# A hybrid state space and attention block: the small matmuls of a state space group stand in three portions behind whole weight pieces, and the combination of the dilations takes four steps a head pair

## The chip, the core and the metric

The kernel runs on one NeuronCore of a Trainium2 chip. The time is device microseconds from launch to the last output, the median of repeated runs. The core's engines are TensorE (PE in the profile, PEld for its weight loads), VectorE (DVE), ScalarE (ACT), GpSimd (POOL) and SyncE (SP), which issues most DMAs. Each runs its own list of instructions in order and waits on semaphores for the others.

## The reference

One layer on 512 tokens of width 1024, in fp32. A wide projection feeds a state space branch and an attention branch; both are gated and summed, then come an output projection and a gated feed-forward net. Cut to what the change touches:

```python
xbc = silu(causal_dwconv(xbc, conv_w, conv_b))          # gives xs, B, C
X = (xs * dt).reshape(b, c, Q, G, K, P)                  # 4 chunks of 128 tokens, 8 groups of 4 heads
a_cs = cumsum(dt * A)
CB = einsum('bclgn,bcsgn->bcgls', C, B)
y_diag = einsum('bcgkls,bcsgkp->bclgkp', CB * Ldec, X)   # Ldec: decay between two tokens of a chunk
states = einsum('bclgn,bcgkl,bclgkp->bcgkpn', B, decay_states, X)
prev = scan over chunks of: carry * chunk_decay + states
y_off = einsum('bclgn,bcgkpn,bcgkl->bclgkp', C, prev, exp(a_cs))
y = rms_norm((y_diag + y_off + d_skip * xs) * silu(z))   # per group of 256 channels

# attention: three dilations (1, 4, 16), 8 heads each
wts = softmax(stack(lses), axis=0)
o = einsum('gbsh,gbshd->bshd', wts, stack(outs))         # the combination of the dilations
```

## The kernel before

**Precision by split.** Each fp32 product of a weight and an activation runs as three products of rounded parts: weight high by activation high, high by low, low by high (`mm_chan`, `proj_tok`, `mm_tok`). ScalarE rounds a weight piece to `whi` (line 105), VectorE subtracts for `wlo` (line 106). Weights come in pieces of 512 KB (`raw`, three buffers; `whi` and `wlo` have three each). A piece of the state space stage is 24 matmuls of 128x512, 8 for each of the three products, into a bank `ps_ssd` of the four `mm` banks.

**Large and small work.** The state space stage has 8 groups of 6 pieces: B, C, two of x, two of z. What a group then needs of TensorE beside its pieces, the small work, is in the generator `ssd_side`: `ps_cb` (C by B, 4 matmuls), `ps_bt` (3 transposes of B), `ps_xt` (two banks of 4 transposes of x), `ps_st` (3 matmuls for the states), then for each half j of the group `ps_y` (8 matmuls with 64 columns of weights, the part within a chunk) and `ps_o` (3 matmuls, the part from the state before), and `ps_n` (2 matmuls that sum squares). On the other engines it makes `xdt` and `xdc` (x by time step and by decay, from `ps_xt`), `cbm` (from `ps_cb`, masked), `btok`, `prev` (the running state), the decay matrix in `bc` (a 1 MB load, a subtraction, Relu, Exp, then times `cbm`), y in `ysb`, and `sq`, `sr`, `vv`, `rv` for the norm. After the eighth group come the gates (`ps_gate`, 16 pieces, of which six still carry the last group's small work), the two branch projections (`ps_ap`, `ps_sp`), the output projection and the feed-forward net.

**What sets the order.** TensorE's list is in the order of the code. `tick()` resumes each waiting generator once; there is a tick after the 12th matmul of a piece, inside `mm_chan`, and one at its end. `yield n` in a generator lets n ticks pass. So the numbers in `G0`, `G1`, `GN` (groups 0, 1, and all others), `YL` and `NL` say at which half piece each bit of small work stands. ScalarE's and VectorE's lists are set in this stage by the framework's scheduler from its own estimates. Small work uses the PSUM tags `tr` and `aux`, two banks each; a bank is free again when its reader is done. `bc` and `eb` have two buffers, so `load_decay(g + 2)` (line 777) has to wait until group g's `ps_y` and y are done.

**The combination.** `combine()` weighs the three dilations' outputs for 4 pairs of heads and writes `ah` and `al`, the split input of `ps_ap`. It runs beside the first groups, one tick after the cast to `ah` and one after `al`, so two ticks a pair.

Of the kernel before, what the change touches and what calls it, by code (L numbers as in the profile page):

```python
# [38 lines left out]
def kernel(  # L39
# [6 lines left out]
    nc = tc.nc  # L46
# [556 lines left out]
    def combine():  # L603
# [37 lines left out]
        for j in range(4):  # L641
# [10 lines left out]
            yield 1  # L652
# [43 lines left out]
    def ssd_side(g, bct, xst, zs, at):  # L696
# [12 lines left out]
        yield at["cb"]  # L709
# [7 lines left out]
        btok = T("btok", [P, 3, P])  # L717
        ps = bank("tr", f"ps_bt{g}")
        for c in range(3):
            nc.tensor.transpose(ps[:, c * P:(c + 1) * P], bct[:, 0, c * P:(c + 1) * P], ident)  # L720
        nc.scalar.copy(btok.rearrange("p c n -> p (c n)"), ps[:, :3 * P])
# [3 lines left out]
        xdt = T("xdt", [P, NT, 4, 64])
        xdc = T("xdc", [P, 3, 4, 64])
        for hf in range(2):
            ps = bank("tr", f"ps_xt{g}_{hf}")
            for c in range(2):
                for j in range(2):  # L730
                    o = c * 256 + j * P
                    t0 = (2 * hf + c) * P
                    nc.tensor.transpose(ps[:, o:o + P], xst[:, j, t0:t0 + P], ident)
            p4 = ps.rearrange("p (c h d) -> p c h d", c=2, h=4)
            cc = slice(2 * hf, 2 * hf + 2)
            nc.vector.tensor_mul(xdt[:, cc], p4, dtt[:, cc, hs].unsqueeze(3).broadcast_to((P, 2, 4, 64)))
            n = 2 - hf
            cc = slice(2 * hf, 2 * hf + n)
            nc.vector.tensor_mul(xdc[:, cc], p4[:, :n], dtd[:, cc, hs].unsqueeze(3).broadcast_to((P, n, 4, 64)))
            yield 1  # L740
# [16 lines left out]
        for j in range(2):  # L757
            b = 2 * g + j
            y = ysb[:, b, :]
            psy = bank("aux", f"ps_y{g}_{j}")  # L760
# [5 lines left out]
            pso = bank("aux", f"ps_o{g}_{j}")  # L766
# [9 lines left out]
            yield YL - j  # L776
# [7 lines left out]
        ps = bank("aux", f"ps_n{g}")  # L784
# [17 lines left out]
    normal = dict(zip(("cb", "x", "y"), GN))  # L802
# [6 lines left out]
    for g in range(8):  # L809
        if g > 1:  # L810
            branch_tiles(g)
        if g > 1:
            start(ssd_side(g, *tiles[g], normal), G2W if g == 2 else 0)
        banks = []
        for i in range(6):
# [19 lines left out]
            if (g, i) == (0, 4):  # L835
# [588 lines left out]
```

## Time and profile before

| | |
|---|---|
| median of 3 runs | 1204.27 us (1204.27 to 1204.46) |
| the profiled execution, span within it | 1204.23 us, 1202.3 us |
| busy: TensorE, its weight loads | 1196.1 us (99%), 997.8 us (83%) |
| busy: VectorE, ScalarE, GpSimd | 753.7 us (63%), 575.4 us (48%), 170.5 us (14%) |
| granted clock of TensorE | 0.999 |
| state space pieces, first and last matmul | 263.8 and 595.0 us |
| share of `ps_ssd` in the chain that ended last | 22% |

The busy table gives for each engine the time in which at least one of its instructions runs. The chain that ended last is followed back from the end of the program, at each step to what released it; a row of it has a start, a length and what ran. Rows of the timeline have a start, a length, the engine, the line, output and inputs with their shape, how many instructions were merged, and in brackets how long the engine sat idle before and what ended that. A plain fp32 matmul leaves two records, so `ps_cb L714 x8` is 4 matmuls.

### The profile page before, as it was taken

To read this page: it belongs to the slowest core of one execution; us is meant where nothing else is said; L and a number is where in the kernel's file an instruction comes from. 1 tells how busy PE (TensorE), PEld (TensorE's weight loads), DVE (VectorE), ACT (ScalarE), POOL (GpSimd) and SP (SyncE) were. 2 spreads that over 40 slices of the span, in tenths; PEclk is the share of its full clock that TensorE was granted. 3 is DMA by queue.
4 is the path that set the end of the run, shared out by engine and by line. 5 is a ranking of instruction groups with operands and counts; after the bars stand their busy time and mean duration, and the time that the engine had idled before them with its cause. 6 is when DMAs were issued, how large, how long until landed. Compare 5 with 4: busy or idle time off the path is not lost.

```text
span 1202.3 us, 15963 instructions
## 1 busy us (share of the span) xinstructions
PE 1196.1 (99%) x6316; PEld 997.8 (83%) x6316; DVE 753.7 (63%) x999; ACT 575.4 (48%) x890; POOL 170.5 (14%) x143
## 2 busy tenths in 40 slices
PE   9999999999999999999999999999999999999998
PEld 7877778987888888888888888888888989988887
DVE  6224544467789986877644354654788887885542
ACT  5434565467845657456433324433554445454331
POOL 1034422300000201101011000000223232400000
PEclk9999999999999999999999999999999999999999
DMA  5455544322646444434325332344333332334330
GB/s 187 123 124 128 114 103 107 91 66 74 184 124 200 122 134 124 123 97 115 87 72 144 119 103 90 105 142 157 123 108 103 105 107 85 109 95 168 112 116 35
DMA packets 174955, 138.95 MB, mean 116 GB/s; under 512 B 11552, under 2 KB 149584, under 8 KB 173857
## 3 DMA queue, kind: packets, MB, share of 16 engines
q1 hardware_dynamic: 172001, 131.35, 37.6%
q0 software_dynamic: 2880, 6.59, 2.4%
q8 instruction: 49, 0.80, 0.3%
q14 instruction: 25, 0.20, 0.1%
HBM read 133.22 MB, written 4.70 MB: 115 GB/s over the span
## 4 chain that ended last, share of the span: by engine, by line
PE 99%; ACT 0%; DVE 0%; issue 0%; POOL 0%; DVEq 0%
PE ps_ssd L145 22%; PE ps_qk L145 11%; PE ps_u L1282 10%; PE ps_wd L952 10%; PE ps_gate L145 7%; PE ps_sp L919 7%; PE ps_v L409 6%; PE ps_wo L952 3%; PE ps_ua L1108 2%; PE ps_uc L1108 2%; PE ps_ub L1108 2%; PE ps_u L145 2%; PE ps_ap L145 2%; PE ps_s L537 1%; PE ps_y L764 1%; PE ps_pv L579 1%
## 5 line engine op out<-in xcount | busy, mean ns | idle before, releaser
L106 DVE TENSOR_TENSOR wlo<-raw,whi 128x1024 fp32r<-128x1024 f32 x154 | 194.3, 1263 | 315.2 <-ACT whi L105 217.1
L105 ACT CAST whi<-raw 128x1024 fp32r<-128x1024 f32 x154 | 161.7, 1051 | 308.3 <-PE ps_ssd L145 63.1
L145 PE MATMUL ps_ssd<-hl,whi 128*128 128x512 f32 x384 | 102.9, 397 | 0.0
L145 PE MATMUL ps_ssd<-hh,whi 128*128 128x512 f32 x384 | 98.4, 398 | 0.0
L145 PE MATMUL ps_ssd<-hh,wlo 128*128 128x512 f32 x384 | 95.4, 390 | 0.0
L952 PE MATMUL ps_wd<-whi,asp 128*128 128x512 f32 x336 | 89.8, 389 | 0.0
L145 PEld LDWEIGHTS ps_ssd<-hh,wlo 128*128 128x128 f32 x384 | 72.1, 188 | 15.9
L145 PEld LDWEIGHTS ps_ssd<-hh,whi 128*128 128x128 f32 x384 | 70.6, 188 | 14.0 <-issue 0.2
L145 PEld LDWEIGHTS ps_ssd<-hl,whi 128*128 128x128 f32 x384 | 70.2, 188 | 14.1 <-issue 0.2
L952 PEld LDWEIGHTS ps_wd<-whi,asp 128*128 128x128 f32 x336 | 63.1, 188 | 13.1
L952 PE MATMUL ps_wd<-wlo,asp 128*128 128x512 f32 x168 | 51.7, 389 | 0.0
L556 ACT ACTIVATE s<-s,st 128x128 f32<-128x128 f32 (+1 forms) x96 | 39.8, 417 | 21.6 <-DVE st L550 15.7
L145 PE MATMUL ps_qk<-hh,whi 128*128 128x512 f32 x192 | 49.3, 398 | 0.0
L1156 ACT ACTIVATE facc<-facc 128x512 f32<-128x512 f32 x22 | 13.9, 632 | 71.7 <-DVE facc L52 71.6
L145 PE MATMUL ps_qk<-hl,whi 128*128 128x512 f32 x192 | 47.4, 389 | 0.0
L145 PE MATMUL ps_qk<-hh,wlo 128*128 128x512 f32 x192 | 47.4, 389 | 0.0
L1092 DVE TENSOR_TENSOR ulo<-rawup,uhi 128x1024 fp32r<-128x1024 f32 x31 | 43.5, 1404 | 5.2 <-ACT uhi L1086 5.2
L778 POOL TENSOR_TENSOR sq<-sq 128x512 f32<-128x512 f32 x8 | 12.4, 1550 | 240.5 <-ACT sq L775 240.5
L145 PEld LDWEIGHTS ps_qk<-hh,whi 128*128 128x128 f32 x192 | 35.0, 188 | 12.1 <-issue 3.8
L1282 PE MATMUL ps_u<-h2h,uhi 128*128 128x512 f32 x176 | 43.7, 390 | 0.0
L1282 PE MATMUL ps_u<-h2h,ulo 128*128 128x512 f32 x176 | 43.5, 389 | 0.0
L1282 PE MATMUL ps_u<-h2l,uhi 128*128 128x512 f32 x176 | 43.5, 389 | 0.0
(321 smaller groups left out, 2530.0 us busy)
## 6 DMA issues: line engine op xcount, KB each, us to landing
raw<-in_w_in_dram SPq DMA_DIRECT2D x100, 512.0 KB
rawup<-in_w_up_dram SPq DMA_DIRECT2D x40, 512.0 KB
raw<-in_w_down_dram SPq DMA_DIRECT2D x22, 512.0 KB
bc<-scr_a SPq DMA_DIRECT2D x8, 1024.0 KB
raw<-in_w_ssd_proj_dram SPq DMA_DIRECT2D x16, 512.0 KB
hrb<-scr_q POOLq DMA_DIRECT2D x12, 512.0 KB, 6.7
eb<-scr_e SPq DMA_DIRECT2D x16, 256.0 KB
raw<-in_w_out_dram SPq DMA_DIRECT2D x8, 512.0 KB
```

Of the source, the lines that this page charges most:

```text
L105: nc.scalar.copy(hi, raw)
L106: marks["lo"] = nc.vector.tensor_sub(lo, raw, hi.bitcast(F32))
L145: nc.tensor.matmul(ps[:, t0:t0 + nt], a[:, k, c:c + n], b[:, k, t0:t0 + nt], start=(i == 0), stop=(i == total - 1))
L409: nc.tensor.matmul(pss[b], tok(g, kq * 2 + k, b, xx), w[:, k, :], start=(kq == 0 and j == 0 and k == 0), stop=(kq == 3 and j == 2 and k == 1))
L556: nc.scalar.activation(s[:, o:o + nk * P], s[:, o:o + nk * P], AF.Exp, bias=st[:, q, 0, 2 * j + h:2 * j + h + 1], accum_out=st[:, q, 1, 2 ...
L778: nc.gpsimd.tensor_add(sq[:, 0, :], sq[:, 0, :], sq[:, 1, :])
L919: nc.tensor.matmul(pss[j], w[:, k, cs], ys[k][xi], start=(k2 == 0 and i == 0 and k == 0), stop=(k2 == 7 and i == 2 and k == 1))
L952: nc.tensor.matmul(pss[b], xs(k0 + k, i)[:, b * P:(b + 1) * P], ww[:, k, :], start=(k0 == 0 and j == 0 and k == 0), stop=(k0 == nk - 2 and ...
L1092: nc.vector.tensor_sub(lo, source(m, x), hi.bitcast(F32))
L1108: nc.tensor.matmul(ba[m][bk][:, c * H:(c + 1) * H], a[:, k, :], b[:, k, :], start=(i == 0), stop=(i == 11))
L1156: nc.scalar.activation(facc[m], facc[m], AF.Silu)
L1282: nc.tensor.matmul(pss[i], a[:, k, :], b[:, k, :], start=(n == 0), stop=(n == 23))
```

## The change

The small work of a group goes in three portions, each behind a whole piece: first `ps_bt`, both `ps_xt` and `ps_cb`; one piece later `ps_st`; two pieces later both halves of `ps_y` and `ps_o` with no tick between them. For that the second `ps_xt` bank and the second half's `ps_y` and `ps_o` take banks of the other tag, and so does `ps_n`. `xdc` is made ahead of `xdt`. `ps_n` comes at the end of a piece too, just ahead of the next group's `ps_st`. The combination waits three ticks after `ah`, so four ticks a pair. No instruction of a computing engine is added or left out.

```diff
-G0, G1, GN = (2, 1, 1, 1), (5, 2, 4, 2), (7, 2, 2)
-G2W, YL = 4, 3
-NL = (1, 3, 2, 1)
+G0, G1, GN = (3, 4, 1), (10, 4, 2), (12, 4)
+NL = (2, 3, 2, 1)
...
             nc.scalar.copy(ah[:, j, :], acc)
-            yield 1
+            yield 3
             nc.vector.tensor_sub(al[:, j, :], acc, ah[:, j, :].bitcast(F32))
             yield 1
...
-        yield at["cb"]
+        yield at["a"]
+        btok = T("btok", [P, 3, P])
+        ps = bank("tr", f"ps_bt{g}")
+        for c in range(3):
+            nc.tensor.transpose(ps[:, c * P:(c + 1) * P], bct[:, 0, c * P:(c + 1) * P], ident)
+        nc.scalar.copy(btok.rearrange("p c n -> p (c n)"), ps[:, :3 * P])
+        xdt = T("xdt", [P, NT, 4, 64])
+        xdc = T("xdc", [P, 3, 4, 64])
+        for hf in range(2):
+            ps = bank(("tr", "aux")[hf], f"ps_xt{g}_{hf}")
...
+            nc.vector.tensor_mul(xdc[:, cc], p4[:, :n], dtd[:, cc, hs].unsqueeze(3).broadcast_to((P, n, 4, 64)))
+            cc = slice(2 * hf, 2 * hf + 2)
+            nc.vector.tensor_mul(xdt[:, cc], p4, dtt[:, cc, hs].unsqueeze(3).broadcast_to((P, 2, 4, 64)))
         cbm = T("cbm", [P, NT, P])
         ps = bank("aux", f"ps_cb{g}")
...
         yield 1
         nc.vector.tensor_mul(m4, m4, cbm.unsqueeze(1).broadcast_to((P, 4, NT, P)))
-        yield at["x"]
...
+        yield 1
         prev = T("prev", [P, 3, 4, 64])
...
-            psy = bank("aux", f"ps_y{g}_{j}")
+            psy = bank(("aux", "tr")[j], f"ps_y{g}_{j}")
...
-            pso = bank("aux", f"ps_o{g}_{j}")
+            pso = bank(("aux", "tr")[j], f"ps_o{g}_{j}")
...
             nc.scalar.activation(sq[:, j, :], y, AF.Square)
-            yield YL - j
+        yield 3
         load_decay(g + 2)
...
-        ps = bank("aux", f"ps_n{g}")
+        ps = bank("tr", f"ps_n{g}")
...
-            start(ssd_side(g, *tiles[g], normal), G2W if g == 2 else 0)
+            start(ssd_side(g, *tiles[g], normal))
```

How this moves instructions is shown at three places of a late group. The number behind a tile's name is a running number of the buffer, which differs between the two programs; `hh` and `hl` are the activation's high and low part.

First, TensorE's list around the transposes and the states. Before, from the end of a group's last piece into the next group's first (a group's second `ps_xt` and the `ps_n` of the group ahead of it stand inside a piece):

```order
L145 MATMUL ps_ssd_5_4550<-hh,wlo_4457 128x512 x8
L733 MATMUL ps_xt_0_4584<-ident,xst_4282 128x128 x4
L145 MATMUL ps_ssd_0_4594<-hh,whi_4509 128x512 x8
L145 MATMUL ps_ssd_0_4594<-hl,whi_4509 128x512 x4
L785 MATMUL ps_n_4613<-sr_4546,ones_r 1x512
L786 MATMUL ps_n_4613<-sr_4546,ones_r 1x512
L733 MATMUL ps_xt_1_4619<-ident,xst_4282 128x128 x4
L145 MATMUL ps_ssd_0_4594<-hl,whi_4509 128x512 x4
L145 MATMUL ps_ssd_0_4594<-hh,wlo_4510 128x512 x8
L745 MATMUL ps_st_0_4645<-xdc_4583,btok_4526 128x256 x2
L745 MATMUL ps_st_1_4646<-xdc_4583,btok_4526 128x256
```

And after, from the end of a group's first piece to the end of its second:

```order
L144 MATMUL ps_ssd_0_4258<-hh,wlo_4200 128x512 x8
L712 MATMUL ps_bt_4299<-ident,bct_3945 128x128 x3
L722 MATMUL ps_xt_0_4306<-ident,xst_3946 128x128 x4
L722 MATMUL ps_xt_1_4313<-ident,xst_3946 128x128 x4
L733 MATMUL ps_cb_4321<-bct_3945 128x128 x4
L144 MATMUL ps_ssd_1_4329<-hh,whi_4232 128x512 x8
L144 MATMUL ps_ssd_1_4329<-hl,whi_4232 128x512 x8
L144 MATMUL ps_ssd_1_4329<-hh,wlo_4233 128x512 x8
L783 MATMUL ps_n_4365<-sr_4277,ones_r 1x512
L784 MATMUL ps_n_4365<-sr_4277,ones_r 1x512
L743 MATMUL ps_st_0_4372<-xdc_4305,btok_4298 128x256 x2
L743 MATMUL ps_st_1_4373<-xdc_4305,btok_4298 128x256
```

Four places of small work (with `ps_cb` and `ps_bt`, which stood a piece earlier still) became two, and `ps_st` stands one piece behind all of the transposes and `ps_cb`.

Second, TensorE's list around y. Before, the two halves stand a piece and a half apart:

```order
L764 MATMUL ps_y_0_4387<-bc_3893,xdt_4272 64x128 x8
L769 MATMUL ps_o_0_4396<-bct_3971,prev_4334 128x128 x3
L145 MATMUL ps_ssd_2_4405<-hh,whi_4299 128x512 x8
L145 MATMUL ps_ssd_2_4405<-hl,whi_4299 128x512 x8
L145 MATMUL ps_ssd_2_4405<-hh,wlo_4300 128x512 x8
L145 MATMUL ps_ssd_3_4441<-hh,whi_4362 128x512 x8
L145 MATMUL ps_ssd_3_4441<-hl,whi_4362 128x512 x4
L764 MATMUL ps_y_1_4460<-bc_3893,xdt_4272 64x128 x8
L769 MATMUL ps_o_1_4469<-bct_3971,prev_4334 128x128 x3
```

After, they follow each other at the end of the fourth piece:

```order
L144 MATMUL ps_ssd_3_4420<-hh,wlo_4345 128x512 x8
L762 MATMUL ps_y_0_4458<-bc_3926,xdt_4304 64x128 x8
L767 MATMUL ps_o_0_4467<-bct_3945,prev_4371 128x128 x3
L762 MATMUL ps_y_1_4476<-bc_3926,xdt_4304 64x128 x8
L767 MATMUL ps_o_1_4485<-bct_3945,prev_4371 128x128 x3
L144 MATMUL ps_ssd_4_4494<-hh,whi_4397 128x512 x8
```

The same four pieces of small work stand at one place instead of two.

Third, VectorE's list between a group's transposes and its states (`wlo` is the split of a later weight piece, `bct` on line 52 or 51 a tap of the next group's convolution, `bc<-bc,cbm` the decay matrix times `cbm`). Before:

```order
L715 TENSOR_TENSOR cbm_4209<-ps_cb_4210,triu 128x512
L52 SCALAR_TENSOR_TENSOR xst_3972<-ps_ssd_3_4131,sc,xst_3972 128x509
L723 TENSOR_TENSOR bc_3893<-bc_3893,cbm_4209 128x2048
L106 TENSOR_TENSOR wlo_4256<-raw_4253,whi_4255 128x1024
L736 TENSOR_TENSOR xdt_4272<-ps_xt_0_4274,dtt 128x512
L739 TENSOR_TENSOR xdc_4273<-ps_xt_0_4274,dtd 128x512
L106 TENSOR_TENSOR wlo_4300<-raw_4297,whi_4299 128x1024
L736 TENSOR_TENSOR xdt_4272<-ps_xt_1_4309,dtt 128x512
L739 TENSOR_TENSOR xdc_4273<-ps_xt_1_4309,dtd 128x256
L106 TENSOR_TENSOR wlo_4363<-raw_4360,whi_4362 128x1024
```

After:

```order
L704 TENSOR_TENSOR bc_4546<-acs,bc_4546 128x2048
L105 TENSOR_TENSOR wlo_4543<-raw_4540,whi_4542 128x1024
L105 TENSOR_TENSOR wlo_4584<-raw_4581,whi_4583 128x1024
L105 TENSOR_TENSOR wlo_4655<-raw_4652,whi_4654 128x1024
L51 SCALAR_TENSOR_TENSOR bct_4565<-ps_ssd_0_4568,sc,bct_4565 128x511
L726 TENSOR_TENSOR xdc_4615<-ps_xt_0_4616,dtd 128x512
L51 SCALAR_TENSOR_TENSOR bct_4565<-ps_ssd_0_4568,sc,bct_4565 128x510
L728 TENSOR_TENSOR xdt_4614<-ps_xt_0_4616,dtt 128x512
L51 SCALAR_TENSOR_TENSOR bct_4565<-ps_ssd_0_4568,sc,bct_4565 128x509
L726 TENSOR_TENSOR xdc_4615<-ps_xt_1_4623,dtd 128x256
L728 TENSOR_TENSOR xdt_4614<-ps_xt_1_4623,dtt 128x512
L734 TENSOR_TENSOR cbm_4630<-ps_cb_4631,triu 128x512
```

The five operations on `ps_xt` and `ps_cb` stand in a row behind the next decay's subtraction and three weight splits, with the taps of a convolution between them.

On ScalarE's list the same decay's Relu, a table load and Exp follow the subtraction, then a copy and a cast, a table load and the Silu of `zs`, another cast, and the scaling that starts the convolution:

```order
L706 ACTIVATE bc_4546<-bc_4546 128x2048
L707 ACT_TABLE_LOAD
L707 ACTIVATE bc_4546<-bc_4546 128x2048
L829 COPY zs_4257<-ps_ssd_5_4527 128x512
L104 CAST whi_4583<-raw_4581 128x1024
L797 ACT_TABLE_LOAD
L797 ACTIVATE zs_4257<-zs_4257 128x1024
L104 CAST whi_4654<-raw_4652 128x1024
L676 ACTIVATE bct_4565<-ps_ssd_0_4568,sc 128x512
L713 COPY btok_4608<-ps_bt_4609 128x384
```

Before, at the same place of ScalarE's list:

```order
L707 ACTIVATE bc_4203<-bc_4203 128x2048
L105 CAST whi_4255<-raw_4253 128x1024
L799 ACTIVATE xst_3972<-xst_3972 128x1024
L831 COPY zs_3973<-ps_ssd_4_4184 128x512
L708 ACT_TABLE_LOAD
L708 ACTIVATE bc_4203<-bc_4203 128x2048
L105 CAST whi_4299<-raw_4297 128x1024
L831 COPY zs_3973<-ps_ssd_5_4240 128x512
L799 ACT_TABLE_LOAD
L799 ACTIVATE zs_3973<-zs_3973 128x1024
```

One cast, one Silu and one copy no longer stand between the Relu and the Silu of `zs`.

More of the change, by code (lines that the diff above doesn't have):

```diff
@@ L708, in ssd_side @@
         nc.scalar.activation(mt, mt, AF.Exp, scale=-1.0)
-        yield at["cb"]
+        yield at["a"]
[8 more added lines that the diff above has]
+            ps = bank(("tr", "aux")[hf], f"ps_xt{g}_{hf}")
+            for c in range(2):
+                for j in range(2):
+                    o = c * 256 + j * P
+                    t0 = (2 * hf + c) * P
+                    nc.tensor.transpose(ps[:, o:o + P], xst[:, j, t0:t0 + P], ident)
+            p4 = ps.rearrange("p (c h d) -> p c h d", c=2, h=4)
+            n = 2 - hf
+            cc = slice(2 * hf, 2 * hf + n)
+            nc.vector.tensor_mul(xdc[:, cc], p4[:, :n], dtd[:, cc, hs].unsqueeze(3).broadcast_to((P, n, 4, 64)))
+            cc = slice(2 * hf, 2 * hf + 2)
+            nc.vector.tensor_mul(xdt[:, cc], p4, dtt[:, cc, hs].unsqueeze(3).broadcast_to((P, 2, 4, 64)))
         cbm = T("cbm", [P, NT, P])
@@ L716, in ssd_side @@
                              triu.unsqueeze(1).broadcast_to((P, NT, P)))
[L717 to L721, printed above, removed]
         yield 1
         nc.vector.tensor_mul(m4, m4, cbm.unsqueeze(1).broadcast_to((P, 4, NT, P)))
-        yield at["x"]
[L725 to L740, printed above, removed]
+        yield 1
         prev = T("prev", [P, 3, 4, 64])
@@ L800, in silus @@
         yield 1
-    normal = dict(zip(("cb", "x", "y"), GN))
+    normal = dict(zip(("a", "y"), GN))
     tiles = {}
@@ L844 @@
                 load_decay(1)
-                start(ssd_side(0, *tiles[0], dict(zip(("cb", "x", "y"), G0))), G0[3])
+                start(ssd_side(0, *tiles[0], dict(zip(("a", "y"), G0))), G0[2])
             if (g, i) == (0, 5):
-                start(ssd_side(1, *branch_tiles(1), dict(zip(("cb", "x", "y"), G1))), G1[3])
+                start(ssd_side(1, *branch_tiles(1), dict(zip(("a", "y"), G1))), G1[2])
                 start(silus(*tiles[0]), 1)
```

## The prediction

> **What bounds the kernel now.** I read the page's busy table first, then the chain of work that ended last over one group of the state space stage, then starts of single instructions on TensorE in that stage.
>
> ```profile
> span 1202.3 us, 15963 instructions
> PE 1196.1 (99%) x6316; PEld 997.8 (83%) x6316; DVE 753.7 (63%) x999; ACT 575.4 (48%) x890; POOL 170.5 (14%) x143
> ```
>
> TensorE is busy for all but 6.2 us of the span, so the change can gain only by making TensorE's own work shorter, and can lose by making it wait. The profiled execution took 1204.23 us, 1.9 us more than its span; the median of the runs is 1204.27, so sums against the one hold for the other. The next fence is the chain from one group's `ps_cb` to the next group's (start in us, length in us, what), and behind it two rows of the same view from later on.
>
> ```profile
> 464.46 0.89 PE ps_cb L714 x8
> 465.36 0.33 PE ps_bt L720 x3
> 465.68 8.20 PE ps_ssd L145 x36
> 473.88 0.44 PE ps_xt L733 x4
> 474.32 2.77 PE ps_ssd L145 x12
> 477.08 0.23 PE ps_n L785
> 477.32 0.23 PE ps_n L786
> 477.55 0.44 PE ps_xt L733 x4
> 477.99 2.77 PE ps_ssd L145 x12
> 480.75 1.30 PE ps_st L745 x6
> 482.05 5.46 PE ps_ssd L145 x24
> 487.51 1.02 PE ps_y L764 x16
> 488.54 0.86 PE ps_o L769 x6
> 489.40 8.20 PE ps_ssd L145 x36
> 497.60 1.02 PE ps_y L764 x16
> 498.63 0.86 PE ps_o L769 x6
> 499.49 5.49 PE ps_ssd L145 x24
> 504.98 0.89 PE ps_cb L714 x8
> ...
> 635.14 54.43 PE ps_gate L145 x240
> 689.57 21.76 PE ps_ap L145 x96
> ```
>
> A group takes 504.98 - 464.46 = 40.52 us, and every step of it is on TensorE: nothing else stands in the chain. 240 matmuls without any small work take 54.43 us, 0.2268 each. The group's 144 large matmuls would take 32.66 at that rate; they take 8.20 + 2.77 + 2.77 + 5.46 + 8.20 + 5.49 = 32.89. The 0.23 too much lies on six returns from small work to large, 0.04 each. The small work is the other 7.62 us.
>
> **What a place of small work costs beyond its own steps.** A transpose takes 0.44 / 4 = 0.11, and a record of `ps_cb` 0.89 / 8 = 0.11 (a plain fp32 matmul leaves two records). At 0.11 a step, `ps_y` (16 records, two side by side, so 8 steps) should take 0.89 and takes 1.02; `ps_o` (6 records) should take 0.67 and takes 0.86. So each `ps_y`, `ps_o` pair pays 0.13 + 0.19 = 0.32. `ps_cb`, `ps_bt`, `ps_xt` and `ps_st` (6 records twice as long, 1.30) pay nothing of the sort. The starts say where the first part comes from:
>
> ```profile
> 485.54 1.97 PE L145 MATMUL ps_ssd<-hh,wlo 128*128 128x512 f32 x8
> 487.44 1.09 PE L764 MATMUL ps_y<-bc,xdt 128*64 128x128 f32 x16
> ...
> 503.91 1.07 PE L145 MATMUL ps_ssd<-hl,whi 128*128 128x512 f32 x4
> 504.82 1.05 PE L714 MATMUL ps_cb<-bct 128*128 128x128 f32 x8
> ```
>
> Eight large matmuls ahead of `ps_y` last 1.90 from start to start, against 8 x 0.2268 = 1.81; four ahead of `ps_cb` last 0.91, just 4 x 0.2268. The price hangs on the change of the stationary's width, 128 columns to 64 and back, not on the interruption.
>
> **The change part by part.**
>
> *Fewer interruptions.* In the order of instructions the small work of the eight groups stands at 52 places before and at 27 after. 25 returns at 0.04 go: 25 x 0.04 = -1.0 us. The bounds of one return are 0.02 (the 5.46 row against 24 x 0.2268) and 0.05 (the 2.77 rows), so -0.5 to -1.3.
>
> *`ps_bt`, both `ps_xt` and `ps_cb` together, `ps_n` ahead of `ps_st`.* The same instructions at the same 128 columns: their own time stays, 0.
>
> *Both halves of y together.* Before, a half goes large, `ps_y`, `ps_o`, large: the width changes twice a half, four times a group. After it goes large, y, o, y, o, large: it changes four times again. The new step is from `ps_o` to `ps_y`, which no row shows. At the low end it is free (then the entry's 0.13 goes: 8 x -0.13 = -1.0), at the high end it costs the 0.19 of `ps_y` to `ps_o` (0.06 more than now: 8 x 0.06 = +0.5). I take the entry's 0.13, since large to `ps_y` is the same step from 128 columns to 64: 0.
>
> The Trainium skill, page "TensorEngine Tiling (Array Packing)", section Key Properties, says that changing the tiling mode drains the engine, while changing the tile alone does not. By that rule the merged halves save nothing, as here; the trace agrees, with 0.09 us ahead of `ps_y` and none ahead of `ps_cb`.
>
> *Waits that the new order could bring.* The state portion now needs the whole first portion's vector work, one piece after it. The longest way to it is this: the second half's `ps_y` frees the decay buffer, SP loads the next decay, VectorE subtracts, ScalarE does Relu, a table, Exp, a table, Silu and two weight casts, VectorE the last weight split, three taps of a convolution and the five operations on `ps_xt` and `ps_cb`; `ps_st` also takes the two banks that these free. Rows of before for its parts, by SP, VectorE and ScalarE:
>
> ```profile
> 458.16 0.33 SPq L689 DMA_DIRECT2D bc<-scr_a  x1
> ...
> 464.30 2.37 DVE L705 TENSOR_TENSOR bc<-acs,bc 128x2048 f32<-128x2048 f32 x1 [0.57 <-DMA bc<-scr_a]
> 466.59 0.74 DVE L52 SCALAR_TENSOR_TENSOR xst<-ps_ssd,sc,xst 128x510 f32<-128x510 f32 x1
> ...
> 474.36 0.69 DVE L736 TENSOR_TENSOR xdt<-ps_xt,dtt 128x512 f32<-128x512 f32 x1 [2.44 <-PE ps_xt L733]
> 474.96 0.68 DVE L739 TENSOR_TENSOR xdc<-ps_xt,dtd 128x512 f32<-128x512 f32 x1
> 475.56 1.22 DVE L106 TENSOR_TENSOR wlo<-raw,whi 128x1024 fp32r<-128x1024 f32 x1
> ...
> 478.63 0.41 DVE L739 TENSOR_TENSOR xdc<-ps_xt,dtd 128x256 f32<-128x256 f32 x1
> ...
> 466.70 1.92 ACT L707 ACTIVATE bc<-bc 128x2048 f32<-128x2048 f32 x1 [0.50 <-DVE bc L705]
> 468.52 1.03 ACT L105 CAST whi<-raw 128x1024 fp32r<-128x1024 f32 x1
> 469.46 1.05 ACT L799 ACTIVATE xst<-xst 128x1024 f32<-128x1024 f32 x1
> 470.42 0.56 ACT L831 COPY zs<-ps_ssd 128x512 f32<-128x512 f32 x1
> ...
> 476.93 1.06 ACT L799 ACTIVATE zs<-zs 128x1024 f32<-128x1024 f32 x1
> ```
>
> The load takes 464.30 - 458.16 = 6.14 (VectorE was waiting for it); from the subtraction to Relu 2.40; ScalarE from 466.70 to 477.99 is 11.29, of which one cast, the `xst` Silu and one copy (1.03 + 1.05 + 0.56 = 2.64, by length) stand elsewhere in the new order: 8.65. Then a cast 1.03, the split 1.22, three taps 3 x 0.74 = 2.22, and 0.68 + 0.69 + 0.41 + 0.69 and `cbm` (taken as `xdt`, the same shape) 0.69 = 3.16. Sum 24.8 us. TensorE takes from the end of that `ps_y` to the new `ps_st`: 0.86 + two pieces 10.92 + a piece 5.44 + the first portion (0.33 + 0.44 + 0.44 + 0.89 = 2.10) + a piece with a return 5.48 + `ps_n` 0.46 = 25.3. So 0.5 is left with every part laid end to end. The rows overlap on an engine (474.36 to 474.96 is 0.60 for 0.69 long), which gives about 1 us more over a dozen parts. I take no wait: 0, with 0 to 1 us in each of about three groups as the bounds. What is queued behind the waiting subtraction on VectorE is three weight splits, each needed a piece or more later.
>
> *The combination of the dilations.* Four ticks a head pair instead of two: 4 x 2 = 8 ticks, four pieces, some 23 us later. The rows are the combination's last operation, and a stretch by engine (stretch, its length, then busy time of TensorE, weight loads, VectorE, ScalarE, GpSimd).
>
> ```profile
> L653 DVE TENSOR_TENSOR al<-ysb,ah x4: 677/680/1776, 374.0 to 398.3; 128x512 fp32r<-128x512 f32 x4
> ...
> 383.00:424.00 41.00, 41.00 (x212) 33.95 (x212) 39.19 (x54) 24.35 (x28) 6.98 (x3) 1.00 0.55 150
> ```
>
> Its last result comes at 398.3 and is read by `ps_ap` at 689.57, so the delay costs nothing: 0. VectorE is busy 39.19 of 41.00 us there and TensorE still never waited, so thinning that out gains nothing either. The last group's sum of squares (`ps_n` for group 7) keeps two pieces behind its y portion: no cost.
>
> **Sum.** 1204.2 - 1.0 + 0 + 0 + 0 = 1203.2 us, within the 0.2% (2.4 us) that a measurement of this kernel can tell from no change.
>
> **Rivals.** *Each place of small work has a price of its own, widths or not.* For it: both parts of the 0.32 could be the cost of entering fp32 work. Against it: `ps_cb` and `ps_xt` enter it free. Then the merged halves save 8 x 0.32 = 2.6 and the returns 1.0: 1200.6 us. *The state portion waits (slower).* Place: `ps_st` of the steady groups, behind the chain above. It decides once that chain is more than 0.5 to 1.5 us longer than I sum it, for example because the load shares the queues with weight loads. If it is 3 us longer, TensorE waits 2 us in each of three groups: 1204.2 - 1.0 + 6.0 = 1209.2; at 2.2 us longer, 1206.8. *The returns stay.* If the 0.04 belongs to the instructions and not to the return, nothing is gained: 1204.2.
>
> **How the numbers follow.** Widths priced as now, returns saved, 1203.2: 0.57. Returns stay: 0.15. Each place has its price: 0.16. State portion waits: 0.12. The range has the first rival in it and stops below most of the waiting one: 1200.6 to 1205.8; the likeliest case's own, from the bounds of the returns and of the new `ps_o` to `ps_y` step, is 1204.2 - 1.3 - 1.0 = 1201.9 to 1204.2 - 0.5 + 0.5 = 1204.2. Faster by over 0.2% is the first rival, 0.16; slower the second, 0.12; the rest, 0.72, is within 0.2%.
>
> **What would show it.** In the chain of the changed kernel a steady group should be about 40.4 us, the first portion 2.1, `ps_n` with `ps_st` 1.76 and the y portion 3.76; 3.1 there would speak for the first rival. TensorE's idle time should stay at 6.2 us, and no row of TensorE should wait for `cbm` or `xdt`; one that does makes me wrong.

## The result and the profile after

The changed kernel takes 1207.73 us, the median of 8 runs (1206.21 to 1209.16), beside 1204.47 us for the kernel before (8 runs). The ratio is 1.0024, 95% interval [1.0013, 1.0035]: it is slower by about 3.3 us. A second set of runs later gave 1208.46 beside 1204.81, ratio 1.0033 [1.0021, 1.0045]. The prediction, 1203.2 and "within 0.2%", was wrong. The time lies where the rival "the state portion waits" put it, though the waits were not quite those it described, as shown below.

The profiled execution took 1209.16 us, the longest of its set, so its sums stand 1.4 us above the median. Some 0.7 us of its distance to the profile before lie ahead of all changed work: the first `ps_ssd` matmul starts at 264.54 and not at 263.85. The busy table, answering to the first fence of the prediction:

```profile
span 1207.3 us, 15957 instructions
PE 1198.6 (99%) x6316; PEld 1001.1 (83%) x6316; DVE 747.3 (62%) x999; ACT 574.3 (48%) x890; POOL 178.0 (15%) x143
```

TensorE's idle time is 8.7 us (1207.3 - 1198.6) and was 6.2. The chain of work that ended last, over one group late in the stage (start, length, what):

```profile
523.88 0.33 PE ps_bt L712 x3
524.20 0.87 PE ps_xt L722 x8
525.08 0.89 PE ps_cb L733 x8
525.97 5.49 PE ps_ssd L144 x24
531.46 0.23 PE ps_n L783
531.70 0.23 PE ps_n L784
531.92 1.29 PE ps_st L743 x6
533.22 10.90 PE ps_ssd L144 x48
544.12 1.02 PE ps_y L762 x16
545.14 0.86 PE ps_o L767 x6
546.01 1.02 PE ps_y L762 x16
547.03 0.86 PE ps_o L767 x6
547.90 16.34 PE ps_ssd L144 x72
564.24 0.33 PE ps_bt L712 x3
```

A group without a wait is 564.24 - 523.88 = 40.36 us, as forecast (40.4); its three portions are 2.09, 1.75 and 3.76 us (forecast 2.1, 1.76, 3.76). Nearly all the loss is in groups 2, 3 and 4 (groups are counted from 0). The same chain from group 3's second `ps_y` to group 4's `ps_st`, cut to its longer rows, shows the wait that I had taken as 0:

```profile
462.54 9.29 DMA bc<-scr_a
471.85 2.42 DVE bc L704
474.29 1.92 ACT bc L706
...
477.52 1.92 ACT bc L707
...
483.13 1.04 ACT whi L104
484.20 1.23 DVE wlo L105
...
488.92 0.61 DVE xdt L728
489.67 1.97 PE ps_st L743 x6
```

Every link is one that the prediction's chain named, in its order. The load alone is 9.29 us where I had put 6.14. In this stage TensorE's list of waits was empty before and now has one row (what waits, for what, us in total, times, longest), and the timeline by stretches shows what followed it (stretch, its length, busy time of TensorE, weight loads, VectorE, ScalarE, GpSimd, then TensorE's granted clock):

```profile
PE ps_st L743 <- DVE xdt L728: 2.5, 2, 1.9
```

```profile
489.00:490.00 1.00, 0.34 (x2) 0.34 (x3) 1.00 (x2) 0.00 (x0) 0.00 (x0) 1.00 0.01 2
490.00:491.00 1.00, 1.00 (x6) 0.83 (x4) 0.97 (x2) 0.00 (x0) 0.00 (x0) 0.81 0.06 2
491.00:492.00 1.00, 1.00 (x4) 0.81 (x3) 1.00 (x1) 0.00 (x0) 0.53 (x1) 0.50 0.08 17
493.00:494.00 1.00, 1.00 (x4) 0.71 (x4) 1.00 (x3) 0.00 (x0) 0.32 (x1) 0.50 0.00 0
```

After the 1.9 us wait TensorE ran at half clock for about 3.4 us, so that its 3.4 us did the work of 1.7. The busy table does not show this, since TensorE counts as busy at half clock too.

For the account I took the time from the first `ps_ssd` matmul to the first `ps_ap`, and in it each stretch from `ps_n` (or `ps_st` where that stands alone) to the next large matmul. Where nothing waits, `ps_n` and `ps_st` take 1.57 us; here 2.68 (group 2), 2.02 (group 3) and 3.94 (group 4). The stage is 425.56 us before and 429.89 after, +4.33. A kernel with the new places and no wait (E6 below) has 424.15. So: -1.41 from the new places, +3.93 for the three waits (matmuls of `ps_st` at half clock included), +0.3 for smaller ones, +1.50 for large matmuls at half clock.

### The profile page after: what moved, and what is told of

Read it like the earlier page. It is cut to its first block, busy times and chain, and to the rows that moved or that the text cites. A ratio compares the mean times of both kernels' runs of the same rounds, so it can differ in the third digit from the quotient of the medians.

```text
span 1207.3 us, 15957 instructions
## 1 busy us (share of the span) xinstructions
PE 1198.6 (99%) x6316; PEld 1001.1 (83%) x6316; DVE 747.3 (62%) x999; ACT 574.3 (48%) x890; POOL 178.0 (15%) x143
## 4 chain that ended last, share of the span: by engine, by line
PE 90%; DVE 3%; ACT 3%; DMA 1%; issue 1%; POOL 1%; POOLq 0%; DVEq 0%; ACTq 0%
PE ps_ssd L144 15%; PE ps_qk L144 11%; PE ps_u L1280 10%; PE ps_wd L950 10%; PE ps_gate L144 7%; PE ps_sp L917 7%; PE ps_v L408 6%; PE ps_wo L950 3%; PE ps_ua L1106 2%; PE ps_uc L1106 2%; PE ps_ub L1106 2%; PE ps_u L144 2%; PE ps_ap L144 2%; DMA bc<-scr_a 1%; PE ps_s L536 1%; PE ps_pv L578 1%
## 5 line engine op out<-in xcount | busy, mean ns | idle before, releaser
L144 PE MATMUL ps_ssd<-hl,whi 128*128 128x512 f32 x384 | 96.4, 391 | 0.0
L776 POOL TENSOR_TENSOR sq<-sq 128x512 f32<-128x512 f32 x8 | 20.5, 2561 | 218.2 <-ACT sq L773 218.2
```

Source lines behind the costliest of these rows:

```text
L144: nc.tensor.matmul(ps[:, t0:t0 + nt], a[:, k, c:c + n], b[:, k, t0:t0 + nt], start=(i == 0), stop=(i == total - 1))
L776: nc.gpsimd.tensor_add(sq[:, 0, :], sq[:, 0, :], sq[:, 1, :])
```

## The experiments

"Wait" is what `ps_n` with `ps_st` took over 1.57 us in the profile, by group. Medians are in us, with the kernel before run on the same chip beside each. The profile is of one execution only: that of E8 took 1204.93 us, 2.4 less than the median, that of E14 1.8 less, and that of E7 2.3 more (its mean granted clock was 0.949). E1 to E4 look for the place of the loss, E5 to E10 move single pieces of work, E11 and E12 ask for the price of a wait, and E13 to E16 test what could speak against the cause found.

| run | median | before | ratio, 95% interval | waits in the profile |
|---|---|---|---|---|
| changed | 1207.73 | 1204.47 | 1.0024 [1.0013, 1.0035] | 1.11, 0.45, 2.37 (groups 2, 3, 4) |
| E1 decay later | 1207.17 | 1205.0 | 1.0014 [1.0005, 1.0023] | 4.5 (group 2) |
| E2 before, longer combination | 1204.61 | 1205.0 | 0.9997 [0.9989, 1.0006] | none over 0.25 |
| E3 changed, shorter combination | 1208.84 | 1205.0 | 1.0035 [1.0021, 1.0049] | 4.5 (group 2) |
| E4 norm's transfers on GpSimd | 1206.37 | 1205.0 | 1.0013 [1.0004, 1.0022] | 0.25, 0.48, 2.06, 0.46 (groups 2 to 5) |
| E5 three edits | 1203.26 | 1204.68 | 0.9987 [0.9979, 0.9996] | none |
| E6 sums on VectorE | 1203.48 | 1204.68 | 0.9988 [0.998, 0.9997] | none |
| E7 E1 with E4 | 1203.12 | 1204.68 | 0.9986 [0.9977, 0.9996] | none |
| E8 E1 with E6 | 1207.36 | 1204.68 | 1.002 [1.0011, 1.0028] | 2.2 (group 2) |
| E9 one sum on VectorE | 1203.73 | 1205.2 | 0.9989 [0.998, 0.9998] | none over 0.14 |
| E10 one sum on GpSimd | 1203.5 | 1205.2 | 0.9985 [0.9976, 0.9994] | 0.25 (group 2) |
| E11 waits on purpose | 1218.3 | 1205.2 | 1.0108 [1.0093, 1.0124] | 3.8, 4.25, 5.5 (groups 4 to 6) |
| E12 decay load twice | 1210.2 | 1205.2 | 1.0041 [1.0028, 1.0054] | 4.4 (group 2), and 1.6 ahead of `ps_n` there |
| E13 lists alone | 1205.62 | 1204.81 | 1.0005 [0.9996, 1.0013] | 0.25, 0.46, 1.66 (groups 2, 3, 4) |
| E14 changed again | 1208.46 | 1204.81 | 1.0033 [1.0021, 1.0045] | 0.25, 0.48, 2.34 (groups 2, 3, 4) |
| E15 small products | 1203.79 | 1205.42 | 0.9987 [0.9977, 0.9996] | 0.6, 0.5 (groups 4, 5) |
| E16 cast behind | 1205.99 | 1205.45 | 1.0008 [0.9999, 1.0017] | 1.66, 0.03, 0.76 (groups 2, 3, 4) |

(In the expectations "second group" and "third group" are groups 2 and 3.)

**E1, the decay's chain taken out of the way.**

```diff
-G0, G1, GN = (3, 4, 1), (10, 4, 2), (12, 4)
+G0, G1, GN = (3, 4, 1), (10, 4, 2), (10, 4)
...
-        nc.vector.tensor_sub(m4, ...)
+        with tc.issue_after(marks["cbm"].ins) if g > 1 else ExitStack():
+            nc.vector.tensor_sub(m4, ...)
...
-        nc.vector.tensor_mul(cbm, ...)
+        marks["cbm"] = nc.vector.tensor_mul(cbm, ...)
...
-            start(ssd_side(g, *tiles[g], normal))
+            start(ssd_side(g, *tiles[g], normal), 2)
```

> The changed kernel, with the subtraction on the decay matrix put behind the previous group's cbm in VectorE's list (and so Relu and Exp behind it in ScalarE's list); nothing else moves by hand. Theory A (the state portion waits because the next-but-one group's decay load, subtraction, Relu, Exp and two table loads stand ahead of its own vector work): that chain no longer holds load, subtraction, Relu and Exp, so no TensorE row waits at ps_st; what is left is the saving of the prediction, about 1.0 to 1.3 us, so 1203.2 to 1203.5 beside 1204.5 for the kernel before. Theory B (VectorE and ScalarE are too full in the groups with the combination, the load plays no part): waits of 0.5 to 1 us at ps_st of the second and third group stay, 1205 to 1207. Theory C (the new places of small work cost TensorE more by themselves, waits are a side effect): as the changed kernel, 1207 to 1208.

From group 3 on every wait was gone, as theory A says; but group 2 waited 3.1 us, with a half clock behind it, and the total hardly moved, so the time that theory A forecast was missed. The chain that ended last names another cause there:

```profile
384.72 2.48 POOL rv L793
...
396.62 6.58 DMA raw<-in_w_in_dram
...
403.27 1.05 ACT whi L104
```

GpSimd's power on a 128x4 tile (`rv`) lasted 384.72 to 390.93, 6.2 us against 1.0 to 1.5 in the kernel before. Between the rows shown the chain goes on through GpSimd's sum of squares behind the power, ScalarE's cast to `sr` and a weight cast behind that, VectorE's split, SP's `fb` loads, and at 396.62 the weight load that ScalarE's cast waited for until 403.2. SP itself stood behind the power too, at `scr_r`, which it issued at 390.97. Which of the two ways held the weight load up was not taken apart.

**E2 and E3, the combination.** E2 is the kernel before with this edit, E3 the changed kernel with the reverse.

```diff
             nc.scalar.copy(ah[:, j, :], acc)
-            yield 1
+            yield 3
```

> The kernel before, with the combination's four ticks a pair alone. Theory A and C: no TensorE wait arises, 1204.2 to 1204.7, the same as the kernel before within 0.1%. Theory B': the longer combination, which now reaches into later groups, is itself what costs: 1206 to 1208, with waits at the state portion in the groups in which it runs on.

> The changed kernel with the combination at two ticks a pair again. Theory A: the wait in the group after the combination (1.9 us behind a decay load of 9.3 us) stems from the order of the lists and the bunched weight loads; it stays or moves to an earlier group, 1207 to 1209. Theory B' (the longer combination is what costs): back to 1203 to 1204.

The longer combination alone costs nothing (0.9997), and the shorter one does not cure the changed kernel. In E3 the wait moved to group 2, where GpSimd's sum of squares took 4.3 us.

**E4, the norm's transfers off SP's queue.**

```diff
-        nc.sync.dma_start(scr_v[g], vv)
+        nc.gpsimd.dma_start(scr_v[g], vv)
...
-        nc.sync.dma_start(rv, ...)
+        nc.gpsimd.dma_start(rv, ...)
...
-        nc.sync.dma_start(scr_r[g]..., rv)
+        nc.gpsimd.dma_start(scr_r[g]..., rv)
```

> The changed kernel with the norm's three small transfers (scr_v, rv, scr_r) issued by GpSimd's queue and not by SP's. If the decay load took 9.3 us because SP stood at these and then issued three weight loads in a bunch just ahead of it (theory A1), the weight loads go out as their buffers come free, the decay load takes 5 to 6 us in every steady group, and the wait of 1.9 us with its half clock is gone: 1203.5 to 1205. If the bunching comes from the weight buffers that come free late (theory A2, ScalarE and VectorE behind), the loads stay bunched and it stays at 1207 to 1208.

A miss for A1: weight loads still went out in a bunch (454.5, 456.4, 459.8), the decay load issued at 461.0 took 8.2 us, and group 4 waited 2.06. The time, 1206.37, lies between those of A1 and A2. So SP's standing at these transfers is not by itself why the load is long. But no half clock followed this time (granted clock 1.00 throughout 484 to 495).

**E5 to E8, which of the edits matter.** E6 is one word; E5 is E6 with E1 and E4, E7 is E1 with E4, E8 is E1 with E6.

```diff
-        nc.gpsimd.tensor_add(sq[:, 0, :], sq[:, 0, :], sq[:, 1, :])
+        nc.vector.tensor_add(sq[:, 0, :], sq[:, 0, :], sq[:, 1, :])
```

> The changed kernel with three edits: the decay's subtraction behind the previous group's cbm, the norm's small transfers on GpSimd's queue, and the sum of the squares (sq plus sq) on VectorE and not on GpSimd. Theory A (two kinds of wait at ps_st: the decay chain ahead of the state portion's vector work in the steady groups; in the second and third group GpSimd, which gets no turn while VectorE is full, and what stands behind it on SP and ScalarE): every ps_n with ps_st section takes 1.57 us and the stage 1.37 us less than before, 1203.2 to 1203.8 beside 1204.5 to 1205.0 for the kernel before. Theory B (VectorE alone is too full): the sum of squares adds 0.6 us a group to VectorE, waits of 1 us or more stay in the second and third group, 1205 to 1207.

> The changed kernel with the sum of the squares on VectorE alone. Theory A: the waits of the second and third group (1.1 and 0.45 us in the profile) go or shrink, since no cast on ScalarE waits for GpSimd any longer; the wait behind the decay load in the group after them (2.4 us and a half clock) stays: 1205 to 1206.5. Theory B: slower than the changed kernel, 1207.5 to 1209.

> The changed kernel with the decay's subtraction later and the norm's small transfers on GpSimd's queue; the sum of squares stays on GpSimd. Theory A: GpSimd's slow power no longer holds up SP and with it the weight loads, so the wait of 3.1 us in the second group goes; a wait of up to 1 us behind the slow sum of squares may stay: 1203.5 to 1205. If the weight load's lateness is not SP's doing: a wait of about 3 us stays, 1206.5 to 1207.5.

> The changed kernel with the decay's subtraction later and the sum of squares on VectorE; the norm's transfers stay on SP's queue. Theory A: GpSimd still runs the power (6.2 us against 1.0 to 1.5) while VectorE is full, SP still stands at scr_r ahead of the weight loads, and the wait of about 3 us in the second group stays: 1206 to 1207.5. If it was the sum of squares that made it late: 1203.5 to 1204.5.

E5, E6 and E7 reach the predicted time and beat both kernels. E6 does so with one edit, though theory A had expected the wait behind the decay load to stay. E7 does so with the sum of group 1 still slow on GpSimd (3.8 us), so a slow sum does not do harm in every order of the lists. E8 took the time expected; in its profile the power took 6.7 us and group 2 waited 1.6 us, not about 3. In E6 no wait at `ps_st` is left; the chain at group 4, to set beside the one above (its last row is cut short by the end of the view):

```profile
480.30 5.49 PE ps_ssd L144 x24
485.79 0.23 PE ps_n L783
486.03 0.23 PE ps_n L784
486.26 0.86 PE ps_st L743 x4
```

What the sum on GpSimd did in the changed kernel is seen in the timelines of VectorE, GpSimd and ScalarE there (start, length, engine, line, what; idle time before, and what ended it):

```profile
391.10 2.28 DVE L704 TENSOR_TENSOR bc<-acs,bc 128x2048 f32<-128x2048 f32 x1
396.69 0.69 DVE L652 TENSOR_TENSOR al<-ysb,ah 128x512 fp32r<-128x512 f32 x1 [3.31 <-ACT ah L650]
```

```profile
388.44 6.09 POOL L776 TENSOR_TENSOR sq<-sq 128x512 f32<-128x512 f32 x1 [4.45 <-ACT sq L773]
431.46 3.68 POOL L776 TENSOR_TENSOR sq<-sq 128x512 f32<-128x512 f32 x1 [15.13 <-ACT sq L773]
468.80 1.29 POOL L776 TENSOR_TENSOR sq<-sq 128x512 f32<-128x512 f32 x1 [11.57 <-ACT sq L773]
```

```profile
394.56 0.62 ACT L779 CAST sr<-sq 128x512 fp32r<-128x512 f32 x1 [6.26 <-POOL sq L776]
```

VectorE has no gap until 391.10 + 2.28 = 393.38; the sum ends at 394.53, 1.15 later, though it began at 388.44. The second slow sum ends at 435.14, 1.15 after VectorE's subtraction ended at 433.99. The add itself needs 1.29. So in these two places GpSimd got no turn while VectorE's instructions followed each other, 4.9 us long in the first. ScalarE's next entry, the cast to `sr`, waited 6.26 us for it, and behind it stood the weight cast, Relu, Exp, Silu and the scaling of the taps, all ahead of `xdt`. The chain of the changed kernel shows it: on its way to group 2's `ps_st` it goes through that sum (cut to some of its rows), and on its way to group 3's through the slow sum of 3.68 us at 431.46.

```profile
388.45 6.09 POOL sq L776
...
395.09 1.05 ACT whi L104
...
398.13 1.90 ACT bc L706
...
405.23 0.60 DVE xdt L728
...
407.14 0.70 PE ps_st L743 x2
```

The Trainium skill, page "SBUF — State Buffer", section "SBUF: two separate sides", says that VectorE and GpSimd share one pair of ports as an exclusive lock, held for a whole instruction, when for example a VectorE operation with two inputs in SBUF meets a GpSimd operation that reads SBUF. The trace agrees: the add behind VectorE took 6.09 us and not 1.29, and the other way round VectorE's subtraction behind the add took 3.39 and not 2.28 in E15.

**E9 and E10, one sum each.** E9 has group 1's sum alone on VectorE (the edit below), E10 all but group 1's.

```diff
-        nc.gpsimd.tensor_add(sq[:, 0, :], ...)
+        (nc.vector if g == 1 else nc.gpsimd).tensor_add(sq[:, 0, :], ...)
```

> The changed kernel with the sum of squares of one group alone, group 1, on VectorE; the other seven stay on GpSimd. Theory D (the sum of group 1, which GpSimd takes 6.1 us for while VectorE is full with the combination, is the first cause: ScalarE's casts stand behind its result, the state portion of group 2 comes late, and the later waits, the bunched weight loads and the decay load of 9.3 us follow from it): no or nearly no wait, 1203.3 to 1204.3. Theory E (the decay chain of the steady groups waits by itself, whatever went on in group 2): a wait of about 2 us in group 4 stays, 1205.5 to 1207.

> The reverse: the sums of seven groups on VectorE, that of group 1 alone on GpSimd. Theory D: waits as in the changed kernel, 1206 to 1208. Theory E' (each group's sum counts alike): about one eighth of the way back, 1203.5 to 1204.2.

E9 was as theory D expects: one instruction of 0.7 us on the other engine removes the waits of all three groups, so group 4's wait is a late effect of what happens around group 2 (the framework also moved two casts ahead of `sr` there, see E16). Two of its eleven executions took longer, 1205.66 and 1207.37, where the longest of E6 took 1203.78. The three weight loads ahead of the decay load went out 6.9, 6.4 and 1.6 us before it in E9 and the decay load took 6.6 us; in the changed kernel they went out 4.9, 4.4 and 1.1 us before it, and it took 9.3. E14 and E13, with the same distances as the changed kernel, have 9.6 and 10.3, E4 with 6.5, 4.5 and 1.2 has 8.2; E16 with 5.8, 3.8 and 0.5 has only 7.5, so the distances do not settle it alone. E10 was a miss for theory D: the sum of group 1 took 5.9 us, yet group 2 waited only 0.25 and the later groups not at all, so the slow sum of group 1 is not enough by itself. With the later sums on VectorE the framework had also laid out the lists of group 3 on otherwise, a cast and a split less ahead of `xdt`, so E10 did not tell the sums of the later groups from the lists.

**E11 and E12, the price of a wait, and a longer load.** Both are E6 with one more edit, E11 the first and E12 the second.

```diff
-            nc.vector.tensor_mul(xdt[:, cc], p4, ...)
+            for _ in range({4: 4, 5: 5, 6: 6}.get(g, 1) if hf else 1):
+                last = nc.vector.tensor_mul(xdt[:, cc], p4, ...)
...
-        nc.vector.tensor_mul(cbm, ...)
+        with tc.issue_after(last.ins):
+            nc.vector.tensor_mul(cbm, ...)
```

```diff
-            nc.sync.dma_start(bc, scr_a[hs, :].partition_broadcast(P))
+            for _ in range(2 if g > 1 else 1):
+                nc.sync.dma_start(bc, scr_a[hs, :].partition_broadcast(P))
```

> The changed kernel with all sums of squares on VectorE, and in groups 4, 5 and 6 the last product into xdt written 4, 5 and 6 times over, so that ps_st has to wait there on purpose: by 0.6 us a repeat and by two weight splits that then stand in between, less 2.5 to 2.9 us of slack, that is about 1.5, 2.5 and 3.5 us. Theory F (a wait costs just its length): 1203.5 plus 7.5 is 1211. Theory G (after a wait of about 2 us or more TensorE runs some 3.4 us at half clock, 1.7 us more each time): two or three such stretches, 1214 to 1216, and the profile shows a granted clock of 0.50 behind each wait long enough.

> The changed kernel with all sums of squares on VectorE, and each decay load from group 2 on issued twice in a row into the same buffer (2 MB and not 1 MB, some 4 us longer). If the state portion's margin is the 0.5 to 1.5 us of the prediction: waits of 2.5 to 3.5 us in five groups, with half clocks behind them, 1215 or more. If it is the 2.5 to 2.9 us that stand between the last xdt and ps_st in the kernel with the sums on VectorE: waits of 1 to 1.5 us in four or five groups, 1208 to 1212.

In E11 `ps_st` waited longer than planned, and with each wait the clock fell to 0.50:

```profile
488.24 2.38 PE L745 MATMUL ps_st<-xdc,btok 128*128 128x256 f32 x6 [2.93 <-DVE xdt L729]
533.34 2.90 PE L745 MATMUL ps_st<-xdc,btok 128*128 128x256 f32 x6 [2.86 <-DVE xdt L729]
579.62 2.90 PE L745 MATMUL ps_st<-xdc,btok 128*128 128x256 f32 x6 [4.11 <-DVE xdt L729]
```

```profile
489.00:490.00 1.00, 1.00 (x4) 0.72 (x4) 1.00 (x2) 0.00 (x0) 0.00 (x0) 0.50 0.94 252
...
580.00:581.00 1.00, 1.00 (x3) 0.77 (x3) 1.00 (x3) 0.18 (x1) 0.09 (x1) 0.50 0.08 10
```

The waits add to 9.9 us; the stage grew by 440.26 - 424.15 = 16.1. So some 6.2 us, 2 us a wait on average, came on top, in stretches at half clock: theory G (theory F would give 1203.5 + 9.9 = 1213.4, and 1218.3 was measured). The stretch lasted 3.4 us behind each of the first two waits. In the third the clock fell 2 us into the wait and stayed at half for 6.8 us. E12 did not answer its question. Groups 3 to 7 did not wait at all, though the second load of group 5's decay landed 12.6 us after the first one's issue: the lists, which the framework sets from its own estimates, had a weight cast, a copy and the Silu of `zs` ahead of that decay's Relu on ScalarE, where in E6 they stand behind it. The wait was in group 2, where the power took 7.1 us. What a longer load costs in unchanged lists is left open.

**E13 and E14, the lists alone, and the changed kernel again.** E13 pins a cast ahead of Exp, the next cast behind `btok` and the split behind `cbm`, as E10 had them (`cbm`, `btok` and `hi` mark the last such instruction), and leaves all sums on GpSimd. The edit is shortened here; E14 has none.

```diff
+        with tc.issue_after(marks["btok"].ins):
             nc.scalar.copy(hi, raw)
+        with tc.issue_after(marks["cbm"].ins):
             nc.vector.tensor_sub(lo, raw, hi.bitcast(F32))
...
+        with tc.issue_after(marks["hi"].ins):
             nc.scalar.activation(mt, mt, AF.Exp, scale=-1.0)
```

> The changed kernel with all sums on GpSimd as there; only the lists of ScalarE and VectorE are set otherwise from the third group's state portion on: the next weight cast ahead of Exp, the third cast behind btok, the third weight split behind cbm (so one cast and one split, 1.0 and 1.2 us, stand no longer ahead of xdc and xdt). Theory H (the order of these lists makes the steady groups wait; the slow sum only adds to it in the second group): no wait from group 3 on, 1203.3 to 1205. Theory D' (the slow sums on GpSimd are needed for the waits in whatever order): a wait of 1 to 2 us in group 4 in most executions, 1206 to 1208.

> The changed kernel as it is, for a second profile and more times beside the same runs of the kernel before. If its waits hang on margins of a few tenths of a us, they stand at other groups in this profile (a sum of 3 to 6 us, spread 1206 to 1209). If they are fixed by the order, the same three groups wait by the same amounts within 0.2 us.

In E14 the same three groups wait. Groups 3 and 4 do so by the same amounts, 0.48 and 2.34 (0.45 and 2.37 in the first profile), so these are fixed by the program; group 2 is not, with 0.25 and 1.11. E14's profile has no half clock (1.00 over 488 to 493 after a wait of 2.10 us) and its execution took 1206.68, the shortest of its set; the others took 1207.84 to 1210.39. They left no trace, but their mean granted clocks are on record: 1.0 for the execution of 1206.68, 0.998 for four of the other five and 0.999 for one. A stretch of 3.4 us at half clock takes 0.0014 off the mean over 1205 us, so a half clock in most of the longer ones fits.

E13, with slow sums of 5.9 and 3.7 us, took 0.7 us off group 4's wait and no more. So another order of these lists does not remove the waits; it sets part of their size (theory D' rather than H, though the time lies between the two). E13's median fell by 2.8 us, more than the wait did. All of its eleven executions have a mean clock of 0.999 or 1.0, so a half clock that comes less often after 1.4 us than after 2.1 would explain the rest.

**E15, VectorE given pauses.** The sums of squares stay on GpSimd. This kernel leaves out most of the combination's products and sums for three of the four head pairs, so it is a probe and not a variant to use.

```diff
-                nc.vector.tensor_mul(num, num, fbs[j, g])
+                h = slice(0, S if j == 0 else 64)
+                nc.vector.tensor_mul(num[:, h], num[:, h], fbs[j, g][:, h])
...
-                    nc.vector.tensor_add(acc, acc, num)
+                    nc.vector.tensor_add(acc[:, h], acc[:, h], num[:, h])
```

> The changed kernel with the combination's products and sums of the last three head pairs on 64 of 512 columns (the attention half of the result is left wrong by that); all sums of squares on GpSimd. VectorE has pauses then where group 1's and 2's sums of squares stand. Theory I (GpSimd's sum takes 5.9 and 3.7 us and not 1.3 because VectorE leaves it no turn, and this is where the waits start): both sums near 1.3 us, no wait of more than 0.3 us at ps_st, 1203.2 to 1204. If GpSimd is slow there for another reason, or the waits start elsewhere: the sums stay at 3.5 us or more, or the wait of about 2 us in group 4 stays, 1206 to 1208.5.

```profile
387.27 1.35 POOL L777 TENSOR_TENSOR sq<-sq 128x512 f32<-128x512 f32 x1 [5.17 <-ACT sq L774]
426.29 2.75 POOL L777 TENSOR_TENSOR sq<-sq 128x512 f32<-128x512 f32 x1 [14.43 <-ACT sq L774]
```

```profile
387.38 3.39 DVE L705 TENSOR_TENSOR bc<-acs,bc 128x2048 f32<-128x2048 f32 x1
```

Group 1's sum took 1.35 us, groups 2 and 3 did not wait, and the ratio is about that of E6: theory I in the main. Two things were not as expected: group 2's sum still took 2.75 us, and groups 4 and 5 waited 0.6 and 0.5, more than 0.3. At group 1's sum GpSimd came first, and it was VectorE's subtraction that took 3.39 and not 2.28. The framework's lists changed somewhat here too, so this is not the pause alone.

**E16, only the reader of the sum moved.** The edit is shortened; `hi` marks the last weight cast.

```diff
+        with tc.issue_after(marks["hi"].ins) if g in (1, 2) else ExitStack():
             nc.scalar.copy(sr[:, 0, :], sq[:, 0, :])
```

> The changed kernel, all sums on GpSimd; in groups 1 and 2 alone the cast to sr stands behind the next weight cast in ScalarE's list and not ahead of it (in the lists two casts move by one or two rows, and VectorE's second xdt stands one tap earlier). The steady groups' lists stay as they are. Theory J (the slow sum does harm only through the work that stands behind its reader on ScalarE): the sums still take 3.5 to 6 us, but groups 2 to 4 wait no more than 0.5 us each and the time is 1203.3 to 1204.5. Theory K (the slow sum does harm in another way, by GpSimd, SP or VectorE, or the runs without waits had them away because their lists differ elsewhere): the wait of about 2 us in group 4 stays, 1206 to 1208.5.

```profile
387.04 10.02 POOL L776 TENSOR_TENSOR sq<-sq 128x512 f32<-128x512 f32 x1 [4.65 <-ACT sq L773]
```

```profile
389.41 1.05 ACT L104 CAST whi<-raw 128x1024 fp32r<-128x1024 f32 x1 [2.51 <-PE ps_ssd L144]
...
397.09 0.62 ACT L780 CAST sr<-sq 128x512 fp32r<-128x512 f32 x1 [6.11 <-POOL sq L776]
```

This lies between the two theories. Two casts moved by one or two places take about half of the loss away (the ratio is 1.0008, against 1.0024 and 1.0033 for the changed kernel and 0.9988 for E6) and group 4's wait falls to 0.76, so the way through ScalarE's queue is real. But the casts that come earlier feed VectorE, whose pause of 3.31 us behind the subtraction is gone: the sum grows to 10.0 us, ScalarE waits 6.1 us for it all the same, and group 2 waits 1.66. With these lists, moving the reader is half a cure; moving the sum is the whole one.

## Why the prediction was wrong, and where it was right

*Fewer interruptions*: right in kind, a little small. Without waits the stage is 1.41 us shorter (E6), forecast 1.0 with bounds 0.5 to 1.3, so just outside the bounds.

*Same width together, `ps_n` ahead of `ps_st`, both halves of y*: right. The portions measure 2.09, 1.75 and 3.76, and the step from `ps_o` to `ps_y` costs 0.13 as the entry did. The first rival (3.1 for the y portion) is out, and so is "the returns stay".

*The combination*: right for its length, 0 (E2, in the old order). But that thinning out VectorE's work there "gains nothing either" held in the old order only: in the new one that work is what the sum on GpSimd stands beside (E15).

*Waits that the new order could bring*: this step failed. It said "I take no wait: 0"; three groups wait, 3.9 us in the profile. Two terms of its sum were wrong.

First, the chain was summed from rows of an undisturbed group, with a load of 6.14 us; in group 4 it took 9.29. The row of 6.14 had no weight load issued in the 9 us ahead of it, the one of 9.29 had three within 5 us. The rest of the chain was right: it took 489.53 - 462.54 - 9.29 = 17.70 us, and the prediction has 24.8 - 6.14 less about 1 for overlap, so about 17.7. So the load is the term that was mis-sized, by 3.15 us, and its rival's "for example because the load shares the queues with weight loads" fits what happened, with a wait of 1.9 where the rival had put 2 for 3. That the measured time also lies near the rival's is in part luck: it had 2 us in each of three groups and no half clock; there was one such group, two smaller waits by another way, and 1.5 us at half clock.

Second, the step listed what stands on SP, VectorE and ScalarE and put GpSimd at nothing. In groups 2 and 3 the chain to `ps_st` goes through GpSimd's sums of squares, 6.09 and 3.68 us long. I looked at GpSimd only as 14% busy, and read VectorE's 39.19 of 41.00 us as harmless because TensorE never waited. The kernel before already had such a sum (GpSimd, then ScalarE):

```profile
392.84 3.37 POOL L778 TENSOR_TENSOR sq<-sq 128x512 f32<-128x512 f32 x1 [16.18 <-ACT sq L775]
396.24 0.62 ACT L781 CAST sr<-sq 128x512 fp32r<-128x512 f32 x1 [2.60 <-POOL sq L778]
```

A weight cast stood behind that reader too, but ScalarE waited only 2.60 us, and TensorE not at all. In the new order the sum of the same group takes 6.1 us, ScalarE waits 6.26, and the state portion stands behind. The prediction's own row for `al` had another sign, its longest of 1776 ns beside a shortest of 677: that one ran beside GpSimd's work on `sr`, which took 2.57 us there. With the one sum of group 1 elsewhere (E9) the decay load is 6.6 us and the time is 1203.73, against 1203.2 forecast. How the late start in group 2 makes the load of group 4 long was not taken apart further.

The price of a wait was also too low: I counted its length, and a half clock can come on top. And the rival got 0.12 although its own deciding point, 0.5 to 1.5 us, lay well inside the spread of these loads, 5.2 to 10.3 us in the runs where VectorE waited for one.

## What to carry to other kernels

When work is gathered into fewer places, sum the chain to each place with everything that stands ahead of it in every in-order queue, a nearly idle engine's few instructions too, and price those with their longest row, not the median. A GpSimd add beside a VectorE without pauses can take several times its own length; if a queue that others need stands behind it, try it on VectorE (0.7 us here). Size a load by one that has as many other loads just ahead of it as it will have in the new order. And a wait of TensorE of about 2 us can cost nearly twice its length, since the clock may fall to half with it: 1.9 us brought 3.4 us at half clock, which is 1.7 us more.

## What the runs showed of the hardware

GpSimd beside VectorE: 1.29 us became 3.7 to 10.0 for the sum of squares, and 1.0 became 6.2 to 7.1 for a power on a 128x4 tile. Two sums of the changed kernel ended 1.15 us after VectorE's next pause began, the power of E1 0.9 us after. A pause is not always needed: the sum of E16 ended 1.15 us after one VectorE instruction and delayed the next, which took 1.65 us and not 0.69.

TensorE's granted clock fell to 0.50 with waits of 1.91, 2.86, 2.93, 2.99, 3.08, 3.10 and 4.11 us, and not with 1.42, 1.63, 1.82 and 2.10. It stayed there for 3.4 us each time, with the 4.11 us wait for 6.8. With the wait of 1.91 us it fell only about 1 us after TensorE had started again. The Trainium skill, page "TensorE: Matmul & The Clock Gate", section "Part 1: The HAM clock gate (the "warmup" mystery)", has the clock fall after at least one idle window of about 3.4 us. The time at half clock agrees with that length; the idle time does not: 1.91 us was enough once, and 2.10 us in another execution was not.
